# Sparse attention's value products in batches of two pairs, and the input embedding's side work begun at the first merged branch

## The chip, the core and the metric

The kernel runs on one core of one Trainium2 chip. Its time is device microseconds (us) of one execution. Below, PE is TensorE, DVE is VectorE, ACT is ScalarE, POOL is GpSimd, and SP is SyncE, which issues most DMAs.

## What is computed

A decoder trunk of two layers over 256 tokens of width 1024, in float32. Cut to what the change touches:

```python
for i in range(DEPTH):                       # 2 layers
    a = rmsnorm(h, norm_mix[i])
    proj = a @ w_in[i]                       # pool u | q | k, v | gates | GLA | merge gates
    y_a = pool_mixer(u_pool, ...)
    y_b = nsa_mixer(q_nsa, kv_nsa, g_nsa, positions, ...)   # partial rotary on q and k
    y_c = gla_mixer(...)
    merged = sum over k of sigmoid(g_k) * (y_k @ w_branch[i, k])
    h = h + merged @ w_out[i]
    h = h + square(relu(rmsnorm(h, norm_ffn[i]) @ w_ff1[i])) @ w_ff2[i]
    h = h + sigmoid(rmsnorm(h, norm_ple[i]) @ w_ple_gate[i]) * (p[i] @ w_ple_proj[i])

# inside nsa_mixer, for a head and a block of 128 queries
s = q @ k_sel.T;  o_slc = masked_softmax(s, ...) @ v_sel     # selected blocks
s = q @ kw.T;     o_win = masked_softmax(s, wmask) @ vw      # sliding window
o = g0 * o_cmp + g1 * o_slc + g2 * o_win
```

With 256 tokens every block is selected, so both softmaxes run over all earlier tokens.

## The kernel before

The matmuls with the weights are done in float32r, each as three products of a high and a low half (L1340, L1341, L1342). Weights come in units of 1 MB by DMA on the SP queue (`prefetch`, L181) into three raw buffers. ACT makes the high half (L187) and DVE the low half by a subtraction (L193); the low half frees the raw buffer for the next load.

Before anything is issued, the kernel writes a list `items` of matmul groups and hooks. A loop at the end walks through it, and the order in which it emits instructions is the order of each engine's queue; nothing is reordered later. A hook calls a function at its place in the list. After each pair of slots of a group the loop makes one step of weight preparation (`step`) and calls `pump`.

`pump` (L295) lets the side work advance. Side work is written as generators: `rope_setup` (sine and cosine of the positions, layer 0 only), `pool_gen`, `att_gen`, `gla_gen` and `emb_gen`. Each call of `pump` lowers the counter of every generator by one and then resumes one generator that is due, the first of the list; `yield 3` means that it is due again three calls later. So side generators compete for the calls: when one takes a call, another waits for the next. `finish(name)` runs what is left of one generator at once.

`emb_gen` loads p of the layer (256 KB, L780), yields 9, then transposes it on PE (L786, four transposes) and splits it into halves (`split`: ACT L232, DVE L234). The product with `w_ple_proj` uses it after the branches are merged.

`att_gen` begins, in the function for the last k and v columns, when the gates' columns of both token tiles are there. Its second step transposes k and v (L452); k has by then been rotated by `rotate` (DVE L388 to L390), which needs the table of rope. Its last part runs over `work`, twelve score items: four for token tile 0 with two heads each, eight for token tile 1 with one head each; neighbours are the two kv groups. At step n it does up to three things in this order: `mix`, `turn(n-2)`, `scores(n)`. `scores` makes a 128x512 tile of scores on PE (L569 to L571), its maximum on DVE (L575, L577), four or two exponentials on ACT (L581), and weighs it by the sums and the gate on DVE (L512 to L515). `turn` transposes that tile on PE (L592) and copies it to SBUF. `mix` multiplies the values with the transposed tiles of a pair of items (L615, sixteen instructions on PE for a pair; the first pair of a token tile also begins the sum with the compressed blocks' product, L606).

In layer 0, while rope is computed, the groups of the items "a" and "b" (the GLA output gate) are evacuated by a tanh on ACT and a product on DVE (L851 and L852, L857 and L858). The sine of rope (L380, L381) needs another table on ACT than tanh.

Of the kernel before, what the change touches and what calls it, by code (L numbers as in the profile page):

```python
# [115 lines left out]
def trunk(tc, x, p, positions, norm_mix, w_in, pool_w, pool_scale, cmp_pos_k, cmp_w_k, cmp_pos_v,  # L116
# [10 lines left out]
    with es:  # L127
# [14 lines left out]
        def wt(dt=F32):  # L142
            return wp.tile([128, 512], dt, tag="w", name=nm("w"))

        def ps():
            return pp.tile([128, 512], F32, tag="ps", name=nm("ps"))
# [83 lines left out]
        def split(q, scale=1.0):  # L230
            hi, lo = wt(F32R), wt(F32R)
            act(hi, q, AF.Copy, scale=scale)  # L232
            if scale == 1.0:
                tt(lo, q, hi.bitcast(F32), op=ALU.subtract)  # L234
            else:
                stt(lo, q, scale, hi.bitcast(F32), op0=ALU.mult, op1=ALU.subtract)
            return hi, lo
# [54 lines left out]
        def start(name, gen):  # L292
            sides.append([name, gen, 0])
# [134 lines left out]
        def att_gen(L, i):  # L428
# [128 lines left out]
            work = [(0, g, (2 * a, 2 * a + 1)) for a in range(2) for g in range(2)]  # L557
# [3 lines left out]
            def scores(n):  # L561
                t, g, hs = work[n]
                nk = 128 * (t + 1)
                q = ps()
                for a, hd in enumerate(hs):
                    o = q[:, a * 256:(a + 1) * 256].rearrange("p (b k) -> p b k", b=2) if t == 0 else q
                    A = slice(hd * 128, (hd + 1) * 128)
                    kh, kl = (k.rearrange("p (b k) -> p b k", b=2)[:, :, 0:128] if t == 0 else k for k in kz[g])
                    mm(o, qT[t][0][:, A], kh, start=True, stop=False)  # L569
                    mm(o, qT[t][0][:, A], kl, start=False, stop=False)  # L570
                    mm(o, qT[t][1][:, A], kh, start=False, stop=True)  # L571
                na = 512 // nk
                qv = q.rearrange("p (a k) -> p a k", a=na)
                dv = qv[:, :, nk - 128:nk]
                tt(dv, dv, causal[:, None, :].to_broadcast([128, na, 128]), op=ALU.add)  # L575
                mx = small(4, "mx", 4)
                nc.vector.tensor_reduce(mx[:, 0:na], qv, axis=AX.X, op=ALU.max, negate=True)  # L577
                e = wt()
                c = (g * 4 + hs[0]) * 2
                for a in range(na):  # L580
                    act(e[:, a * nk:(a + 1) * nk], q[:, a * nk:(a + 1) * nk], AF.Exp, bias=mx[:, a:a + 1],  # L581
                        accum_out=sums[t][:, c + a:c + a + 1])
                th = L.gate[t].rearrange("p (n j) -> p n j", j=3)[:, g * 4 + hs[0]:g * 4 + hs[-1] + 1, 1:3]
                weigh(e.rearrange("p (n b k) -> p n b k", n=len(hs), b=2),
                      sums[t][:, c:c + na].rearrange("p (n b) -> p n b", b=2), th)
                st[n] = e

            def turn(n):
                e = st[n]
                q = ps()  # L590
                for a in range(4):
                    nc.tensor.transpose(q[:, a * 128:(a + 1) * 128], e[:, a * 128:(a + 1) * 128], ident)  # L592
                s = wt()
                if n % 2:
                    act(s, q, AF.Copy)
                else:
                    nc.vector.tensor_copy(s, q)
                st[n] = s
# [3 lines left out]
            def mix(n):  # L602
                t, _, hs = work[n]
                if n in (0, 4):
                    oT.append(ps())
                    mm(oT[t], vbd, pbd[t], start=True, stop=False)  # L606
                o = oT[t][:, hs[0] * 128:(hs[-1] + 1) * 128]
                end = n + 2 == len(work) or work[n + 2][0] != t
                for br in range(2):
                    for b in range(t + 1):  # L610
                        for g in range(2):
                            G = slice(g * 64, (g + 1) * 64)
                            s = st[n + g].rearrange("p (n b k) -> p n b k", b=2, k=128)
                            rhs = s[:, :, br] if t == 0 else s[:, br, b]
                            mm(o[G].rearrange("p (n k) -> p n k", k=128) if t == 0 else o[G],  # L615
                               L.v[b][:, 256 + br * 128 + g * 64:256 + br * 128 + (g + 1) * 64], rhs,
                               start=False, stop=end and br == 1 and b == t)
                st[n] = st[n + 1] = None
                if end:
                    L.yB.append([split(oT[t], 0.5)])  # L620

            la, lb = 2, 4
            for n in range(len(work) + lb + 1):
                if n > lb and (n - lb) % 2:
                    mix(n - lb - 1)
                if la <= n < len(work) + la:
                    turn(n - la)
                if n < len(work):
                    scores(n)
                yield 3  # L630
# [147 lines left out]
        def emb_gen(L, i):  # L778
            s = wt()
            load(s.rearrange("q (t c) -> q t c", t=2), p[i, 0].rearrange("(t q) c -> q t c", q=128))  # L780
            yield 9
            q = ps()
            for t in range(2):
                for k in range(2):
                    c = slice(t * 256 + k * 128, t * 256 + (k + 1) * 128)
                    nc.tensor.transpose(q[:, c], s[:, c], ident)  # L786
            L.pT = split(q)


        def layer(i):  # L790
            L = Box()
# [6 lines left out]
            def hook(fn, *a):  # L798
                items.append(Hook(lambda: fn(*a)))
# [104 lines left out]
            else:  # L904
# [4 lines left out]
                items.append(ck[0][1])  # L909
                items.append(cq[1].pop(0))  # L910
                hook(norm_s, 1, kmix)
            hook(lambda: start("emb", emb_gen(L, i)))
            if i == 0:
                hook(lambda: late_start())
            items.extend(cq[1] + ck[1])
# [3 lines left out]
            def feed(c):  # L919
                c0, n, post = feeds[c]  # L920
                for gs in chunk(kmix, two(wi, c0, n), post, n):
                    items.extend(gs)

            def gm(br, ns=(0, 1)):
                for n in ns:
                    for gs in chunk(kmix, two(wi, C_GM + br * D + n * 512), post_gm(br, n)):
                        items.extend(gs)

            def branch(br, name, attr, first, ns=(0, 1)):
                for n in ns:  # L930
                    if br == 1:

                        wr = w_branch[i, br][:, n * 512:(n + 1) * 512].rearrange("(g i d) n -> g d i n", g=2, i=4)
                        u = unit([(slice(g * 64, g * 64 + 64), wr[g]) for g in range(2)])
                    else:
                        u = col_unit(w_branch[i, br], 0, n * 512, 512)
                    for t in range(2):
                        box = Box()

                        def post(t=t, n=n, box=box):  # L940
                            T = L.T[br, t, n]
                            stt(T, T, 1.0, box.ps, op0=ALU.add, op1=ALU.mult)
                            if first:
                                L.T["m", t, n] = T
                            else:
                                m = L.T["m", t, n]
                                tt(m, m, T, op=ALU.add)
                        pairs = [(s, (lambda t=t, s=s: lhs_of(getattr(L, attr)[t], s))) for s in range(4)]
                        items.append(Group(u, pairs, (box, 512), True, True, post))


            for c in SEQ:
                if c in feeds:
                    feed(c)
                elif c in "GHI":
                    gm("GHI".index(c))
                elif c == "g":
                    hook(finish, "pool")
                    branch(0, "pool", "yA", True)
                elif c == "h":  # L960
                    hook(finish, "att")
                    branch(1, "att", "yB", False)
                elif c == "i":
                    hook(finish, "gla")
                    branch(2, "gla", "yC", False)
# [199 lines left out]
        for i in range(DEPTH):  # L1165
            layer(i)
# [144 lines left out]
        for it in items:  # L1311
# [4 lines left out]
            box, n = it.acc  # L1316
# [56 lines left out]
```

## Time and profile before

| | |
|---|---|
| time, median of 3 runs | 917.88 us (917.86 to 918.08) |
| profiled execution | 917.47 us, span 915.7 us |
| mean granted clock of TensorE | 0.997 |
| PE busy | 905.3 us (99%) |
| DVE busy | 672.6 us (73%) |
| ACT busy | 486.2 us (53%) |
| POOL busy | 23.5 us (3%) |
| DMA | 160.02 MB, mean 175 GB/s |

The span is the time from the first to the last instruction that the profiler saw; the execution's own time is 1.8 us longer. Busy times can overlap on PE, since matmuls are pipelined: the distance from one start to the next says what a matmul takes of the span.

### The profile page before, as it was taken

The page shows a single profiled execution, that of the slowest core. Times are in us where ns is not written, and L with a number is a line of the kernel's source. Part 1 is how long each engine was busy: PE and PEld are TensorE (multiplying, and loading weights), DVE is VectorE, ACT ScalarE, POOL GpSimd, SP SyncE. Part 2 cuts the span into 40 slices and gives each one's busy share as a digit, 9 for nine tenths or more (in the row PEclk, how much of TensorE's full clock was granted, in tenths as well). Part 3 has the DMA queues.
Part 4 walks back from the last instruction along what each step waited for, and adds up shares of the span by engine and source line. Part 5 has one row for each costly group of instructions (what it writes and reads, how often), then busy time and mean ns, then how long its engine had stood idle before and what let it go on. Part 6 is the DMA issues. An engine that isn't in the chain of part 4 may idle for free.

```text
span 915.7 us, 12762 instructions
## 1 busy us (share of the span) xinstructions
PE 905.3 (99%) x4865; PEld 760.9 (83%) x4865; DVE 672.6 (73%) x1204; ACT 486.2 (53%) x838; POOL 23.5 (3%) x53
## 2 busy tenths in 40 slices
PE   9999999999999999999999999999999999999996
PEld 6988888788888888888889888878888888888885
DVE  5887877799567766666876877778985776666675
ACT  6665556454464544544665554645445565444553
POOL 1000000000000000000100000000000000000003
PEclk9999999999999999999999999999999999999998
DMA  8696453445535655555358825445553565555531
GB/s 273 198 286 201 138 161 116 121 155 189 180 138 197 229 199 199 187 184 184 99 154 268 238 94 183 139 149 128 163 192 106 180 233 184 184 185 189 197 143 46
DMA packets 92486, 160.02 MB, mean 175 GB/s; under 512 B 11756, under 2 KB 20616, under 8 KB 92424
## 3 DMA queue, kind: packets, MB, share of 16 engines
q1 hardware_dynamic: 92248, 159.13, 52.9%
q8 instruction: 38, 0.62, 0.3%
q14 instruction: 24, 0.20, 0.1%
q10 hardware_dynamic: 176, 0.07, 0.0%
HBM read 158.14 MB, written 1.05 MB: 174 GB/s over the span
## 4 chain that ended last, share of the span: by engine, by line
PE 95%; DVE 3%; DMA 1%; ACT 1%; issue 1%; ACTq 0%; DVEq 0%
PE ps L1340 21%; PE ps L1342 21%; PE ps L1341 21%; PE ps L1328 13%; PE ps L1330 7%; PE ps L615 1%; DVE lo L193 1%; PE ps L592 1%; PE ps L247 1%; DMA raw<-in_w_in 1%; PE ps L571 1%; PE ps L569 1%; PE ps L570 1%; PE ps L227 1%; PE ps L748 1%
## 5 line engine op out<-in xcount | busy, mean ns | idle before, releaser
L193 DVE TENSOR_TENSOR lo<-raw,hi 128x1024 fp32r<-128x1024 f32 (+1 forms) x296 | 340.9, 1179 | 41.7 <-ACT hi L187 39.6
L1340 PE MATMUL ps<-hi,w 128*128 128x512 f32 (+3 forms) x952 | 367.7, 386 | 0.5 <-ACT w L1301 0.5
L1342 PE MATMUL ps<-hi,w 128*128 128x512 f32 (+3 forms) x952 | 359.8, 378 | 0.0
L1341 PE MATMUL ps<-lo,w 128*128 128x512 f32 (+3 forms) x952 | 359.7, 378 | 0.0
L187 ACT ACTIVATE hi<-raw 128x1024 fp32r<-128x1024 f32 (+1 forms) x296 | 291.1, 1025 | 87.0 <-PE ps L1342 31.5
L1342 PEld LDWEIGHTS ps<-hi,w 128*128 128x128 f32 x952 | 178.9, 188 | 34.1
L1340 PEld LDWEIGHTS ps<-hi,w 128*128 128x128 f32 x952 | 179.0, 188 | 33.2 <-issue 1.4
L1341 PEld LDWEIGHTS ps<-lo,w 128*128 128x128 f32 x952 | 179.1, 188 | 30.5 <-DVE lo L1293 0.3
L1328 PE MATMUL ps<-w,hi 128*128 128x512 f32 x512 | 130.4, 392 | 0.0
L1328 PEld LDWEIGHTS ps<-w,hi 128*128 128x128 f32 x512 | 92.1, 189 | 16.3
L1330 PEld LDWEIGHTS ps<-w,lo 128*128 128x128 f32 x512 | 70.0, 190 | 5.1
L1330 PE MATMUL ps<-w,lo 128*128 128x256 f32 x512 | 71.6, 283 | 0.0
L1038 DVE TENSOR_TENSOR w<-w,ps 128x256 f32<-128x256 f32 x64 | 26.9, 420 | 57.3 <-ACT w L1037 57.3
L581 ACT ACTIVATE w<-ps,mx 128x128 f32<-128x128 f32 (+1 forms) x64 | 26.2, 417 | 78.9 <-DVE mx L577 57.5
L1037 ACT ACTIVATE w<-ps 128x256 f32<-128x256 f32 x64 | 24.2, 382 | 57.1 <-PE ps L1328 57.1
L232 ACT ACTIVATE w<-w 128x512 fp32r<-128x512 f32 x36 | 22.8, 632 | 56.2 <-DVE w L1040 50.5
L234 DVE TENSOR_TENSOR w<-w,w 128x512 fp32r<-128x512 f32 x36 | 24.9, 693 | 25.2 <-ACT w L232 25.2
L256 ACT ACTIVATE w<-ps,cols 128x128 fp32r<-128x128 f32 x64 | 17.4, 395 | 33.7 <-PE ps L247 33.7
L232 ACT ACTIVATE w<-ps 128x512 fp32r<-128x512 f32 x22 | 13.1, 596 | 36.2 <-PE ps L227 22.5
L512 DVE TENSOR_SCALAR sums<-sums 128x2 f32<-128x2 f32 (+1 forms) x24 | 4.1, 170 | 31.6 <-ACT w L581 31.6
L258 DVE SCALAR_TENSOR_TENSOR w<-ps,cols,w 128x128 fp32r<-128x128 f32 x64 | 17.3, 343 | 8.5 <-ACT w L256 8.5
L1040 DVE SCALAR_TENSOR_TENSOR w<-w 128x512 f32<-128x512 f32 x32 | 22.1, 692 | 1.1
(231 smaller groups left out, 677.6 us busy)
## 6 DMA issues: line engine op xcount, KB each, us to landing
raw<-in_w_ff SPq DMA_DIRECT2D x64, 1024.0 KB, 5.8
raw<-in_w_in SPq DMA_DIRECT2D x42, 1024.0 KB, 5.2
raw<-in_w_branch SPq DMA_DIRECT2D x8, 1024.0 KB, 5.3
raw<-in_w_out SPq DMA_DIRECT2D x8, 1024.0 KB, 5.1
raw<-in_w_ple_gate SPq DMA_DIRECT2D x8, 1024.0 KB, 5.2
raw<-in_w_in SPq DMA_DIRECT2D x8, 528.0 KB, 3.8
raw<-in_w_branch SPq DMA_DIRECT2D x8, 512.0 KB, 6.1
raw<-in_w_in SPq DMA_DIRECT2D x4, 560.0 KB, 5.2
```

What stands on the lines that cost most here:

```text
L187: act(hi, u.raw[:, a:b, :], AF.Copy)
L193: tt(lo, u.raw[:, a:b, :], hi.bitcast(F32), op=ALU.subtract)
L232: act(hi, q, AF.Copy, scale=scale)
L234: tt(lo, q, hi.bitcast(F32), op=ALU.subtract)
L581: act(e[:, a * nk:(a + 1) * nk], q[:, a * nk:(a + 1) * nk], AF.Exp, bias=mx[:, a:a + 1], accum_out=sums[t][:, c + a:c + a + 1])
L1037: act(zc, q[:, 256:512], AF.Copy)
L1038: tt(zc, zc, q[:, 0:256], op=ALU.add)
L1328: mm(box.ps, w, x, start=(it.first and s == 0), stop=(it.last and s == 3))
L1330: mm(box.ps[:, 0:256], w, x[:, 0:256], start=False, stop=False)
L1340: mm(box.ps, ah, wh, start=(it.first and j == 0), stop=False)
L1341: mm(box.ps, ah, wl, start=False, stop=False)
L1342: mm(box.ps, al, wh, start=False, stop=(it.last and j == last))
```

## The change

Two edits. In `att_gen`, `mix` is called for two neighbouring pairs of score items in one step, four items at a time, at n = 7, 11 and 15, where it was called for one pair at n = 5, 7, 9, 11, 13 and 15. The loop of steps is one shorter. In `layer`, the hook that starts `emb_gen` moves from behind the first q, k and v groups to the first merged branch, ahead of `finish("pool")`. The lines between the two places are numbered one higher after the change.

```diff
@@ -619,10 +619,11 @@
-            la, lb = 2, 4
-            for n in range(len(work) + lb + 1):
-                if n > lb and (n - lb) % 2:
+            la, lb = 2, 6
+            for n in range(len(work) + 4):
+                if n > lb and (n - lb) % 4 == 1:
                     mix(n - lb - 1)
+                    mix(n - lb + 1)
                 if la <= n < len(work) + la:
                     turn(n - la)
                 if n < len(work):
@@ -909,7 +910,6 @@
                 items.append(ck[0][1])
                 items.append(cq[1].pop(0))
                 hook(norm_s, 1, kmix)
-            hook(lambda: start("emb", emb_gen(L, i)))
             if i == 0:
                 hook(lambda: late_start())
             items.extend(cq[1] + ck[1])
@@ -955,6 +955,7 @@
                 elif c in "GHI":
                     gm("GHI".index(c))
                 elif c == "g":
+                    hook(lambda: start("emb", emb_gen(L, i)))
                     hook(finish, "pool")
                     branch(0, "pool", "yA", True)
                 elif c == "h":
```

PE's queue at step n = 5 in layer 0, before. The w tiles of L615 are the values and the turned tiles of items 0 and 1, that of L592 is the weighed tile of item 3, and L569 to L571 are the scores of item 5.

```order
L1342 MATMUL ps_1447<-hi_1259,w_224 128x512
L606 MATMUL ps_1506<-w_811,vbd_973 128x512
L615 MATMUL ps_1506<-w_1333,w_390 64x256
L615 MATMUL ps_1506<-w_1401,w_390 64x256
L615 MATMUL ps_1506<-w_1333,w_390 64x256
L615 MATMUL ps_1506<-w_1401,w_390 64x256
L592 MATMUL ps_1512<-con,w_1413 128x128 x4
L569 MATMUL ps_1519<-w_817,w_899 128x512
L570 MATMUL ps_1519<-w_818,w_899 128x512
L571 MATMUL ps_1519<-w_817,w_900 128x512
```

The same place after the change.

```order
L1343 MATMUL ps_1436<-hi_1248,w_224 128x512
L592 MATMUL ps_1495<-con,w_1402 128x128 x4
L569 MATMUL ps_1502<-w_806,w_888 128x512
L570 MATMUL ps_1502<-w_807,w_888 128x512
L571 MATMUL ps_1502<-w_806,w_889 128x512
```

The products of the first pair have left; the transposes of item 3 stand directly behind the weight matmuls. The first pair now stands at step n = 7, together with the second (items 0 to 3, then the turn of item 5 and the scores of item 7):

```order
L1343 MATMUL ps_1603<-hi_1350,w_157 128x512
L606 MATMUL ps_1627<-w_800,vbd_962 128x512
L615 MATMUL ps_1627<-w_1322,w_390 64x256
L615 MATMUL ps_1627<-w_1390,w_390 64x256
L615 MATMUL ps_1627<-w_1322,w_390 64x256
L615 MATMUL ps_1627<-w_1390,w_390 64x256
L615 MATMUL ps_1627<-w_1448,w_390 64x256
L615 MATMUL ps_1627<-w_1500,w_390 64x256
L615 MATMUL ps_1627<-w_1448,w_390 64x256
L615 MATMUL ps_1627<-w_1500,w_390 64x256
L592 MATMUL ps_1641<-con,w_1509 128x128 x4
L569 MATMUL ps_1648<-w_806,w_888 128x512
```

In layer 1 PE's queue is changed in the same way at both steps. ACT's queue in layer 0, before, from the tanh of L851 for token tile 0. The names rp and rope are the angles and the table of rope, and hi is a high half of weights.

```order
L851 ACTIVATE w_472<-ps_522,st_287 128x248
L187 ACTIVATE hi_590<-raw_533 128x560
L187 ACTIVATE hi_601<-raw_533 128x560
L851 ACTIVATE w_519<-ps_569,st_302 128x248
L187 ACTIVATE hi_617<-raw_554 128x560
L377 ACTIVATE rp_419<-rp_415 128x16
L380 ACT_TABLE_LOAD
L380 ACTIVATE rope<-rp_419 128x2x8
L381 ACTIVATE rope<-rp_415 128x2x8
L187 ACTIVATE hi_634<-raw_554 128x560
...
L828 ACT_TABLE_LOAD
L828 ACTIVATE gate_728<-ps_688,st_287 128x24
```

The same stretch after the change (L852 is the tanh that was L851).

```order
L852 ACTIVATE w_471<-ps_513,st_287 128x248
L187 ACTIVATE hi_581<-raw_524 128x560
L377 ACTIVATE rp_411<-rp_407 128x16
L380 ACT_TABLE_LOAD
L380 ACTIVATE rope<-rp_411 128x2x8
L381 ACTIVATE rope<-rp_407 128x2x8
L187 ACTIVATE hi_596<-raw_524 128x560
L852 ACT_TABLE_LOAD
L852 ACTIVATE w_510<-ps_560,st_302 128x248
L187 ACTIVATE hi_611<-raw_546 128x560
L187 ACTIVATE hi_623<-raw_546 128x560
```

The sine with its table load, which stood behind the second tanh, now stands ahead of it, and the second tanh has a table load of its own. The table load that stood ahead of the gates (L828) is gone.

## Rows read from the trace of the kernel before

**Rows 1.** Waits of TensorE; columns: engine, line, releaser, total us, times, longest.

```profile
PE ps L1234 <- DVE w L1229: 1.5, 1, 1.5
PE ps L1340 <- ACT w L1301: 0.5, 1, 0.5
PE ps L452 <- DVE w L390: 0.2, 1, 0.2
```

**Rows 2.** Timeline of TensorE, 141 to 195 us: start, us, instruction, count.

```profile
141.63 0.60 PE L592 MATMUL ps<-con,w 128*128 128x128 f32 x4
141.98 0.48 PE L569 MATMUL ps<-w,w 128*128 128x512 f32 x1
...
183.06 0.39 PE L1341 MATMUL ps<-lo,w 128*128 128x512 f32 x1
183.29 0.39 PE L1342 MATMUL ps<-hi,w 128*128 128x512 f32 x1
183.61 0.44 PE L748 MATMUL ps<-w,w 128*64 128x128 f32 x4
...
185.19 0.39 PE L751 MATMUL ps<-w,w 128*64 128x128 f32 x4
185.50 0.50 PE L1340 MATMUL ps<-hi,w 128*128 128x512 f32 x1
...
193.01 1.09 PE L615 MATMUL ps<-w,w 128*64 128x128 f32 x16
194.03 0.66 PE L592 MATMUL ps<-con,w 128*128 128x128 f32 x4
```

**Rows 3.** Timeline of TensorE, layer 0, step n=5 of att_gen.

```profile
131.63 1.02 PE L606 MATMUL ps<-w,vbd 128*128 128x512 f32 x2
132.58 1.08 PE L615 MATMUL ps<-w,w 128*64 128x256 f32 x8
133.60 0.66 PE L592 MATMUL ps<-con,w 128*128 128x128 f32 x4
134.01 0.47 PE L569 MATMUL ps<-w,w 128*128 128x512 f32 x1
```

**Rows 4.** Timeline of VectorE: last instructions of items 1, 3 and 11.

```profile
119.31 0.69 DVE L515 TENSOR_TENSOR w<-w,sums 128x512 f32<-128x512 f32 x1
...
132.46 0.69 DVE L515 TENSOR_TENSOR w<-w,sums 128x512 f32<-128x512 f32 x1
...
188.71 0.69 DVE L515 TENSOR_TENSOR w<-w,sums 128x512 f32<-128x512 f32 x1
```

**Rows 5.** Timeline of TensorE, layer 0, turn of item 1.

```profile
120.15 0.63 PE L592 MATMUL ps<-con,w 128*128 128x128 f32 x4
```

**Rows 6.** Timeline of ScalarE, 47 to 61 us; in brackets idle time and releaser.

```profile
47.54 0.47 ACT L851 ACTIVATE w<-ps,st 128x248 f32<-128x248 f32 x1 [3.04 <-DVE a L849]
...
49.88 0.47 ACT L851 ACTIVATE w<-ps,st 128x248 f32<-128x248 f32 x1 [0.75 <-DVE a L849]
...
51.56 0.21 ACT L377 ACTIVATE rp<-rp 128x16 f32<-128x16 f32 x1 [0.65 <-DVE rp L376]
51.79 1.28 ACT L380 ACT_TABLE_LOAD   x1
...
53.31 2.55 ACT L187 ACTIVATE hi<-raw 128x560 fp32r<-128x560 f32 x3
56.90 2.01 ACT L187 ACTIVATE hi<-raw 128x1024 fp32r<-128x1024 f32 x2 [1.03 <-DMA raw<-in_w_in]
```

**Rows 7.** Chain that ended last, 30 to 66 us: start, us, piece.

```profile
32.58 7.05 DMA raw<-in_w_in
...
41.74 0.49 ACT w L232
42.25 0.41 DVE w L234
```

**Rows 8.** Busy time by stretch, 6.0 to 8.4 us; last column GB/s.

```profile
6.00:8.40 2.40, 2.40 (x13) 1.69 (x12) 1.04 (x3) 0.37 (x1) 0.00 (x0) 1.00 1.00 356
```

**Rows 9.** Timeline of VectorE, from 57 us.

```profile
57.12 3.48 DVE L193 TENSOR_TENSOR lo<-raw,hi 128x1024 fp32r<-128x1024 f32 x3
```

## The prediction

> **What bounds the kernel now.** I read the page's first part, then the waits of TensorE (PE), then its timeline from start to start. PE is busy for 905.3 of 915.7 us, and all its waits with a named cause are three, 2.2 us together [rows 1]; two of them are from the start of the program, and the third is in front of L452, the transposes of k and v. So PE's own queue sets the end. An edit counts for the time that it takes from or adds to PE, and for each place where PE comes to an instruction before its operand is there. A busy DVE or ACT is worth nothing by itself, only through the moment at which it hands something to PE. Two places are touched: the steps of att_gen, and the stretch of layer 0 up to L452.
>
> **Fewer batches of value products: -1.8 us.** Three batches in each layer are joined to another one, six in all; the products stay the same. A batch is entered at a price: the first product of a run begins 0.32 us after the last 512-wide matmul (183.29 to 183.61 [rows 2]), whose pitch is otherwise 0.23 (183.06 to 183.29). That is 0.09. Two batches of sixteen take 2 x 1.02 = 2.04 (132.58 to 133.60 [rows 3], and the same for sixteen 128-wide ones, 193.01 to 194.03 [rows 2]); a run of 32 of the same height, eight groups of four in the linear attention (L748 and L751), takes 1.89 (183.61 to 185.50 [rows 2]). That is 0.15. Four transposes behind products take 0.41 (133.60 to 134.01 [rows 3]), alone 0.35 (141.63 to 141.98 [rows 2]): 0.06. Together 0.30 for each of six. If the 0.15 of the run of 32 doesn't carry over to L615, 0.9 is left; more than 2.0 I see no row for. I take 1.8, since the run of 32 has the same form.
>
> **The turn of item 3 loses the work in front of it: +3.4 us.** At n=5 PE did mix(0) and then turn(3). In layer 0 mix(0) filled 131.63 to 133.60, 1.97 us [rows 3]. What turn(3) transposes is the weighed exponential of item 3, and the last instruction that writes it, L515 on DVE, ends at 132.46 + 0.69 = 133.15 [rows 4]: hidden, with 0.45 to spare. With mix(0) gone to n=7, PE stands in front of the transposes at 131.63. How fast a released transpose starts is seen at turn(1), which waits already now: L515 ends at 119.31 + 0.69 = 120.00 [rows 4], L592 starts at 120.15 [rows 5], so 0.15. The wait is 133.15 + 0.15 - 131.63 = 1.67 us, with scores(5) and all of PE's queue behind it. Layer 1 has the same pattern at 580.77 with 0.05 less to spare, which gives 1.72; together 3.4. Nothing in the change brings item 3 forward: its chain on DVE and ACT has the same instructions in the same order, and the products have nothing on either engine until the split at the end. The bounds are 0 (item 3 ready 1.7 us sooner) and 3.9 (all of mix(0), twice). The other two turns that lose a batch in front of them have room: turn(11)'s operand is ready at 188.71 + 0.69 = 189.40 [rows 4] for a start at 194.03 [rows 2], 4.6 us, of which the batch was 1.0; turn(7) has more. The batches that now come later keep four weight tiles for two steps longer, and the pool of 47 has emb's tile less to hold until the branch.
>
> **The side work of the embedding moves: +1.1 and +0.45 us, both in layer 0.** Its four transposes cost PE 0.35, as the four of [rows 2], and 0.1 for the slower first matmul behind them. Before, that lay ahead of L452, where PE waits for DVE, so it was partly free; now it is paid behind. PE comes to L452 0.45 earlier and waits that much longer. In layer 1 there is no such wait, and the place makes no difference. The p load and the split then fall where PE has no wait and the result is needed only at the end of the branches, so I cost them at nothing; without that cover it would be the 0.9 of the split.
>
> The rest comes through rope. Each pump slot runs one due step, and while emb waited in the list it took turns that rope now gets, so rope's last part, with the table load for the sine, moves in front of the second tanh of L851 (the order of ACT above). Before, the load for the sine (51.79, 1.28 us) came behind both tanhs (47.54 and 49.88), and the load back at L828 had room [rows 6]. Now the second tanh has on its path: the first tanh and DVE's work up to the clamp, about 1.5 from 47.54 (0.48, 0.41, and three rope steps of 0.2); L377 0.21; a load of 1.28; the two sines 0.3; one 560-wide high half 0.6; the second load 1.28; its own 0.48. It ends 47.54 + 1.5 + 4.15 = 53.2 instead of 50.35, 2.8 later. From that go two reliefs. The split of emb stood in the chain with 0.49 + 0.41 and a gap of 0.2 [rows 7]; in its place the tanh of L857 of 0.47 is left, so 0.65. And the 256 KB of p were ahead of the 1 MB load that took 7.05 from its issue [rows 7]; at the 356 GB/s that loads side by side reach here [rows 8] they are 0.7, and they delay the load by that if it shares the engines with them throughout. So the second tanh is late by 2.8 - 1.34 = 1.45. Behind it stands the low half that frees a raw buffer, and behind that the load whose landing released ACT at 56.90 [rows 6]. Its low halves are the second and third of the DVE run at 57.12 [rows 9], which had some 0.35 of room. So DVE comes to L390, and PE to L452, 1.1 later. The bounds: 0 (the loads queue otherwise, or the room is larger) and 1.8 (the p load cost the others nothing).
>
> **Sum.** -1.8 + 3.4 + 1.1 + 0.45 = +3.15 on the profiled execution's 917.47, 920.6. That execution lies 0.41 under the median of the runs shown, 917.88; against the median the change gives **921.0**. What a measurement here can tell from no change is 0.2%, 1.84 us: 916.04 to 919.72.
>
> A rule that speaks against the change: a table load here takes 1.28, and the instruction behind it starts without a gap, as that in front ended without one [rows 6]. By the Trainium skill (ScalarE: Activation LUTs, What ACT_TABLE_LOAD costs) a switch costs the load of about 1283 ns and a drain of about 1380 ns besides; the trace agrees with the first number and shows no drain at 51.79. By that rule the sum would be 2.76 higher, since two switches would stand in the chain.
>
> **The rivals.**
> The other side: DVE's lag. DVE and ACT run several us behind PE, and emb's split and load leave the front. If the relief is 1.7 us at turn(3) in both layers, and keeps L452 free as well, both waits are gone: -1.8 - 0.2 [rows 1] = -2.0, 915.9. It decides from 1.67 us on. For it: the split and the load really go. Against it: by the rows they give 1.3 at most, far ahead of 131 us, and the table load takes it back. 0.06.
> Rope is harmless: the move of the sine's table load falls in room that I don't see, and L452 no longer waits, but turn(3) does: -1.8 + 3.4 - 0.2 = +1.4, 919.3, within 0.2%. For it: the first relief is sure; against it: ACT's order, and a chain without gaps from 50 to 65 us. 0.12.
> A switch of tables costs more where ACT has work in flight: by the nearest row as much again as the load, 2 x 1.28, 923.6. Against it: no such gap at 51.79. The page named above has this drain. 0.03.
> The forecast itself has the rest, 0.79, with its own range 919.9 (rope's 1.1 is 0) to 922.3 (rope 1.8, the batches save 1.2).
>
> **How the numbers follow.** The range 919.0 to 922.3 takes in the forecast and the harmless rope and leaves out the other side and the dear switch. Faster by over 0.2% is the other side, 0.06; within it, the harmless rope, 0.12; slower, 0.82.
>
> **What would show it.** Right: in both layers L592 at n=5 waits about 1.7 us for L515; none at turns 7 and 11; runs of 32 value products in about 1.89; on ACT two table loads some 2 us apart near 50 us, the landing that released ACT at 56.90 comes 1 to 2 us later, and L452 waiting 1.5 to 2.5 us for L390; PE's granted clock as before. Wrong: no wait at n=5, which would mean that DVE was not what held turn(3); L452 without a wait; a wait at a place not named here, such as for a raw load behind the emb load at the branch.

## The result and the profile after

The changed kernel takes 922.78 us (median of 6 runs, 921.15 to 924.89); the kernel before took 917.94 beside it (917.16 to 918.47). The ratio is 1.0053, 95% interval 1.0039 to 1.0067: slower by 4.8 us, where +3.15 was forecast, and above the forecast's range. Its single runs are spread over 3.7 us, those of the kernel before over 1.3.

The waits of TensorE (PE) in the changed kernel (engine, line, releaser, total us, times, longest), which answer to [rows 1]:

```profile
PE ps L452 <- DVE w L390: 3.1, 2, 2.7
PE ps L592 <- DVE w L515: 3.1, 2, 1.5
PE ps L1235 <- DVE w L1230: 1.5, 1, 1.5
PE ps L1341 <- ACT w L1302: 0.5, 1, 0.5
```

The two waits that were forecast are there, and no other is new. Now each of them. PE's timeline at step n = 5 in layer 0, then in layer 1, then DVE's at the same place, as [rows 3, 4]:

```profile
136.59 0.39 PE L1343 MATMUL ps<-hi,w 128*128 128x512 f32 x1
138.52 0.63 PE L592 MATMUL ps<-con,w 128*128 128x128 f32 x4 [1.54 <-DVE w L515]
...
586.65 0.39 PE L1343 MATMUL ps<-hi,w 128*128 128x512 f32 x1
588.56 0.63 PE L592 MATMUL ps<-con,w 128*128 128x128 f32 x4 [1.52 <-DVE w L515]
```

```profile
137.68 0.69 DVE L515 TENSOR_TENSOR w<-w,sums 128x512 f32<-128x512 f32 x1
```

From start to start it is 1.93 and 1.91 where a 512-wide matmul takes 0.23, so 1.70 and 1.68 are lost: 3.4, as forecast. L515 ends at 138.37, and the transposes start 0.15 later. The bracket says 1.5, since it counts from the modelled end of the matmul in front: a loss on PE is read from start to start.

The joined batches, in PE's timeline of the changed kernel:

```profile
154.51 1.95 PE L615 MATMUL ps<-w,w 128*64 128x256 f32 x16
156.39 0.66 PE L592 MATMUL ps<-con,w 128*128 128x128 f32 x4
...
185.34 1.97 PE L615 MATMUL ps<-w,w 128*64 128x128 f32 x32
187.24 0.66 PE L592 MATMUL ps<-con,w 128*128 128x128 f32 x4
```

A joined run takes 1.88 and 1.90 to the next start, where two took 2.04; the 0.15 that was forecast is there.

What was underrated is L452. PE's timeline in layer 0, against a start of the transposes at 65.05 and 65.50 before:

```profile
64.14 0.39 PE L1343 MATMUL ps<-hi,w 128*128 128x512 f32 x1
65.01 0.33 PE L452 MATMUL ps<-con,w 128*128 128x128 f32 x1 [0.48 <-DVE w L390]
68.00 0.90 PE L452 MATMUL ps<-con,w 128*128 128x128 f32 x3 [2.66 <-DVE w L390]
...
69.55 0.63 PE L1343 MATMUL ps<-hi,w 128*128 128x512 f32 x1
69.97 0.63 PE L1341 MATMUL ps<-hi,w 128*128 128x512 f32 x1
70.40 0.63 PE L1342 MATMUL ps<-lo,w 128*128 128x512 f32 x1
...
73.81 0.42 PE L1342 MATMUL ps<-lo,w 128*128 128x512 f32 x1
74.07 0.40 PE L1343 MATMUL ps<-hi,w 128*128 128x512 f32 x1
```

Two losses are to be seen. PE stands for 0.64 and 2.90 us (0.87 less 0.23, 2.99 less 0.09), 3.5 where it was 0.35. And behind the wait the same matmuls have a pitch (start to start) of 0.43 in place of 0.23, until 73.8. The stretches of this execution say why (length, busy time of PE, PEld, DVE, ACT, POOL, then the granted clock, DMA share, GB/s):

```profile
66.00:67.00 1.00, 0.00 (x0) 0.00 (x0) 0.97 (x6) 0.62 (x2) 0.00 (x0) 1.00 1.05 403
67.00:67.30 0.30, 0.00 (x0) 0.00 (x0) 0.30 (x4) 0.30 (x1) 0.00 (x0) 0.55 1.04 382
67.30:68.00 0.70, 0.01 (x1) 0.01 (x1) 0.67 (x5) 0.70 (x2) 0.00 (x0) 0.50 1.12 311
68.00:73.40 5.40, 5.40 (x17) 4.42 (x18) 5.37 (x8) 1.24 (x2) 0.00 (x0) 0.50 0.92 182
73.70:75.00 1.30, 1.30 (x9) 1.03 (x9) 1.29 (x4) 0.06 (x1) 0.00 (x0) 0.94 0.86 283
136.00:139.00 3.00, 1.46 (x10) 0.99 (x9) 1.83 (x5) 1.62 (x7) 0.00 (x0) 1.00 1.05 391
586.00:589.00 3.00, 1.48 (x10) 1.00 (x8) 1.79 (x5) 1.66 (x8) 0.00 (x0) 1.00 1.05 391
```

PE's clock went to its lower level, 1.2 for 2.4 GHz, while PE stood at L452, and stayed there until about 73.8, some 6.8 us, with PE busy throughout from 68.00 on. Start by start against the same matmuls in a run at full clock, the 18 pitches from 68.00 on took 2.7 us more. With 3.4 for the turns, 3.2 for L452's standing and -1.7 for the batches this makes 7.6; the profiled span is 7.4 longer (923.1 for 915.7; this execution took 924.89, the longest of the six). At the waits of L592 (last two rows) the clock stayed at its upper level.

ACT's timeline up to the second tanh and the next landing, as [rows 6]:

```profile
43.51 2.01 ACT L187 ACTIVATE hi<-raw 128x1024 fp32r<-128x1024 f32 x2 [0.92 <-DMA raw<-in_w_in]
47.73 0.47 ACT L852 ACTIVATE w<-ps,st 128x248 f32<-128x248 f32 x1 [2.21 <-DVE a L850]
...
49.41 1.28 ACT L380 ACT_TABLE_LOAD   x1
...
51.61 1.28 ACT L852 ACT_TABLE_LOAD   x1
52.91 0.47 ACT L852 ACTIVATE w<-ps,st 128x248 f32<-128x248 f32 x1
...
59.64 2.01 ACT L187 ACTIVATE hi<-raw 128x1024 fp32r<-128x1024 f32 x2 [3.25 <-DMA raw<-in_w_in]
```

The two table loads start 2.2 us apart, each within 0.02 us of the instructions ahead of it and behind it. The second tanh ends at 53.38, 3.0 later than before, where the forecast had 1.45; the landing comes at 59.64, 2.7 later, where it had 1 to 2.

### The profile page after: what moved, and what is told of

The parts are those of the page before. It is cut to its first block, busy times and chain, and to the rows that moved or that the text cites. A ratio compares the mean times of both kernels' runs of the same rounds, so it can differ in the third digit from the quotient of the medians.

```text
span 923.1 us, 12760 instructions
## 1 busy us (share of the span) xinstructions
PE 906.6 (98%) x4865; PEld 763.1 (83%) x4865; DVE 672.9 (73%) x1204; ACT 487.0 (53%) x838; POOL 23.6 (3%) x53
## 4 chain that ended last, share of the span: by engine, by line
PE 95%; DVE 3%; ACT 1%; DMA 1%; issue 0%; ACTq 0%; SPq 0%; DVEq 0%
PE ps L1341 22%; PE ps L1342 21%; PE ps L1343 21%; PE ps L1329 13%; PE ps L1331 7%; PE ps L615 1%; DVE lo L193 1%; PE ps L592 1%; PE ps L247 1%; ACT w L581 1%; PE ps L227 1%; PE ps L571 1%; PE ps L569 1%; PE ps L570 1%; DMA raw<-in_w_in 1%; PE ps L749 1%
```

## The experiments

All times are medians of 5 to 11 runs, with the kernel before run beside them (917.37 beside the first four, 917.67 beside the next four, then 917.46 beside three and 917.63 beside the last).

| run | us | against before | ratio, 95% interval |
|---|---|---|---|
| batches alone | 921.10 | +3.7 | 1.0027 to 1.0054 |
| emb move alone | 921.12 | +3.7 | 1.0023 to 1.0049 |
| emb move, pump calls kept | 917.33 | 0.0 | 0.9989 to 1.0007 |
| batches, later turns | 922.37 | +5.0 | 1.0045 to 1.0070 |
| changed kernel, pump calls kept | 919.16 | +1.5 | 1.0009 to 1.0026 |
| changed kernel, L452's wait filled | 921.90 | +4.2 | 1.0034 to 1.0059 |
| pump calls kept, first pair alone | 917.30 | -0.4 | 0.9986 to 1.0004 |
| pump calls kept, turn of item 3 later | 918.79 | +1.1 | 1.0003 to 1.0021 |
| changed kernel, sine later | 918.86 | +1.4 | 1.0008 to 1.0026 |
| first pair alone, 17 steps | 917.17 | -0.3 | 0.9987 to 1.0004 |
| pump calls kept, scores first at n = 5 | 918.86 | +1.4 | 1.0007 to 1.0024 |
| emb move, L452's wait partly filled | 919.37 | +1.7 | 1.0012 to 1.0030 |

**The two edits apart.** First the batches alone: the changed kernel with the hook of emb put back.

```diff
+            hook(lambda: start("emb", emb_gen(L, i)))
             if i == 0:
                 hook(lambda: late_start())
...
                 elif c == "g":
-                    hook(lambda: start("emb", emb_gen(L, i)))
```

> Only the batches of two pairs; emb starts where it did before. Theory (turn(3) loses its cover, rope's order costs the rest): the joined batches give 1.8, the two waits of L592 cost 1.5 to 1.7 each, so 3.1 to 3.4; sum +1.3 to +1.6, 919.2 to 919.5. L452 waits 0.2 to 0.4 as before, the clock stays at 1.00 from 20 to 900 us, and single runs lie within 1 us. Rival (the batches and the emb move act on each other, or the clock falls at the L592 waits): 921 or more, with a spread of several us.

Measured 921.10, 1.6 over the upper end, where the rival had put it. L592 waits as expected and L452 doesn't, but a wait is new. Its waits:

```profile
PE ps L592 <- DVE w L515: 3.1, 2, 1.6
...
PE ps L227 <- DVE w L770: 0.4, 2, 0.2
```

L227 are the transposes of the linear attention's output. From start to start they lose 1.45 in the two layers. In the kernel before the products of the pair at n = 13 took 1.0 of PE some 2 us ahead of them (193.01 [rows 2]; L227 at 195.92); here these products stand at n = 15, behind them. So a second place lost its cover (the work of PE that hides a wait), which the forecast had not looked at. With emb moved as well L227 doesn't wait (changed kernel, above): PE comes to it at 202.41, for 195.95 here. So the two edits are not additive; which step of emb makes the difference I didn't try. The tail behind the last matmul is 0.7 longer in this profile than in the others, and that stays open too.

The move of emb alone, which is the second half of the change's diff made in the kernel before:

> Only the move of emb; the value products are batched as before. Theory: the sine's table load ahead of the second tanh delays rope, L452 waits 2 to 3.5 us in all, and the granted clock falls behind that wait in some runs, each microsecond at half clock costing half a microsecond: 919.5 to 923.5, single runs spread over 2 us or more, waits of L592 at items 0 and 1 only, as before. Rival (the wait of L452 came with the batches, or the loads just landed late in one run): within 0.5 us of the kernel before.

921.12, as expected, though the runs spread over 1.7 us and not 2 or more; one run of five, with the highest mean clock, took 919.52. PE's timeline and the clock of its profile:

```profile
64.88 0.27 PE L452 MATMUL ps<-con,w 128*128 128x128 f32 x1
67.23 0.55 PE L452 MATMUL ps<-con,w 128*128 128x128 f32 x3 [2.08 <-DVE w L390]
```

```profile
66.00:67.20 1.20, 0.00 (x0) 0.00 (x0) 1.15 (x7) 1.20 (x2) 0.00 (x0) 1.00 1.09 340
67.20:68.40 1.20, 1.17 (x7) 1.04 (x8) 1.20 (x2) 0.59 (x1) 0.00 (x0) 1.00 1.33 248
68.40:71.90 3.50, 3.50 (x12) 2.83 (x11) 3.49 (x5) 0.69 (x1) 0.00 (x0) 0.51 1.30 236
71.90:73.00 1.10, 1.10 (x8) 0.91 (x7) 1.09 (x4) 0.00 (x0) 0.00 (x0) 0.99 1.08 379
```

The clock fell some 1.2 us after PE had gone on, and for some 3.4 us; by the starts that cost 1.6. PE's second start at L452 is 1.7 later than in the kernel before (65.50), where the forecast had 1.1.

**Is it rope's place in ACT's order?** The same move, with an empty generator that takes the two pump calls that emb had.

```diff
+        def pad_gen():
+            yield 9
...
+            if i == 0:
+                hook(lambda: start("pad", pad_gen()))
```

> The move of emb alone, but in layer 0 an empty generator takes the two pump calls that emb took, so ACT's order up to the gates is that of the kernel before, less emb's split. Theory (rope's place in ACT's order is the cause): one table load behind both tanhs and one ahead of the gates, L452 waits under 0.8 us, clock 1.00, 917.4 to 918.6. Rival (emb's own work or load taken out of the front is the cause): L452 waits 2 us or more, 919.5 or more.

917.33, the time of the kernel before. L452 waits 0.4. So neither emb's place nor its work in the front counts; what counts is who gets the pump calls. The same on the changed kernel:

> The changed kernel, but in layer 0 the empty generator takes emb's two old pump calls. Theory: L452 waits under 0.8 us and the clock stays at 1.00, the two waits of L592 at item 3 stay at 1.5 to 1.7, the joined batches give 1.3 to 1.8: 918.6 to 919.6, single runs within 1 us of each other, so 3 to 4 us under the changed kernel. Rival (the L452 wait is a matter of DVE's lag or of the loads): 921 or more.

919.16, in the middle, 3.6 under the changed kernel (3.35 with each against the kernel before beside it), and no wait at L452; the waits of L592 are unchanged:

```profile
PE ps L592 <- DVE w L515: 3.0, 2, 1.5
PE ps L1240 <- DVE w L1235: 1.4, 1, 1.4
PE ps L1346 <- ACT w L1307: 0.5, 1, 0.5
```

Then without the empty generator, only the sine put behind the second tanh again:

In `rope_setup` of the changed kernel:

```diff
+            yield 8
             lim = 3.1415925
             ts(r, r, lim, -lim, op0=ALU.min, op1=ALU.max)
```

> The changed kernel with one yield of 8 calls ahead of rope's last part, so the sine and its table load stand behind both tanhs again, with no empty generator. Theory (the place of the table load, not the pump calls as such, makes L452 wait): L452 waits under 0.8 us, clock 1.00, 918.6 to 919.6, as the run with the old pump calls kept. Rival (other steps of rope or emb's absence from the front make the wait): 921 or more.

918.86, as expected, and L452 waits nowhere. It is the place of rope's last part, the sine with its table load; emb's absence from the front is not the cause. The clamp ahead of the sine moved with it, and the table load by itself was not moved.

**What the wait costs, and what the clock.** Twelve products that nobody reads stand ahead of L452, in the changed kernel.

```diff
+            if i == 0:
+                busy, keep = ps(), aT[("mix", i), 0][0][0]
+                for _ in range(12):
+                    mm(busy, keep[:, 0:128], keep, start=True, stop=True)
             for kv in range(2):
                 src = (L.k, L.v)[kv]
```

> The changed kernel with twelve 128x512 products into an unread PSUM tile ahead of L452 in layer 0, 12 x 0.23 = 2.7 us of TensorE work where it would wait. Theory (the fall of the clock behind the wait is a cost of its own): L452 waits under 1 us, the granted clock stays at 1.00 between 60 and 80 us, 920.0 to 921.5, 1 to 2.5 below the changed kernel although PE does 2.7 us more. Rival (the fall of the clock costs nothing, as PE is ahead of DVE anyway, or it has another cause): 922.5 or more, or half clock as before.

921.90, single runs within 0.4 us (921.62 to 922.04), and the clock at 1.00 throughout. It is 0.4 over the range that I gave, since the products (2.7) were longer than what was left of the wait, which is gone altogether; the time is that of the kernel with the pump calls kept plus the 2.7. The median is 0.9 under that of the changed kernel, 0.6 with each against the kernel before beside it. But two of the six runs of the changed kernel (921.15 and 921.80) are as fast, and the intervals overlap: that useless work makes this kernel faster is not shown. What it plainly does is to narrow the spread, from 3.7 us to 0.4. With six products, on the move of emb alone:

> The move of emb alone, with six 128x512 products into an unread PSUM tile ahead of L452 in layer 0: 6 x 0.23 = 1.4 us, less than the 2.1 us that TensorE waits there without them, so they add nothing to the sum of work and wait. Theory (the fall of the clock is a cost beside the wait): L452 waits 0.5 to 1.2 us, the granted clock stays at 1.00 from 60 to 80 us, 919.3 to 920.0, 1 to 1.6 under the move alone. Rival (the wait alone is the cost): 920.8 to 921.3, as without the products, whatever the clock.

919.37, as expected, 1.75 under the move alone (2.0 with each against the kernel before beside it). The wait was not as expected, though: 1.9, since the first of the four transposes was free and the second stood from 65.33 to 67.48, 2.15 us, nearly the 2.35 without the products. PE's timeline and the clock:

```profile
63.97 1.53 PE L450 MATMUL ps<-w 128*128 128x512 f32 x6
65.33 0.27 PE L456 MATMUL ps<-con,w 128*128 128x128 f32 x1
67.48 0.55 PE L456 MATMUL ps<-con,w 128*128 128x128 f32 x3 [1.88 <-DVE w L390]
```

```profile
66.00:67.00 1.00, 0.00 (x0) 0.00 (x0) 0.96 (x6) 1.00 (x3) 0.00 (x0) 1.00 1.05 383
68.00:69.00 1.00, 1.00 (x6) 0.81 (x5) 1.00 (x2) 0.04 (x1) 0.00 (x0) 1.00 1.19 211
```

L452 goes on 0.25 later than in the move alone, and the kernel is 1.75 faster. That is not the wait, then; it is the clock, which in all eleven runs has a mean of 0.997 or 0.998 (0.995 to 0.997 in the move alone).

**The cover of turn(3).** All turns one step later, with the batches alone:

```diff
-            la, lb = 2, 6
+            la, lb = 3, 6
```

> The batches of two pairs with emb started as before, and every turn one step later (la 3 for 2). Theory: all transposes find their item ready, no L592 wait in either layer; the joined batches' 1.8 stays and the present 0.15 at turn(1) in each layer goes: 915.8 to 916.2. Rival (the later turns only move the wait to the batches or to a tile that is held longer, or the batches give nothing): 917.5 or more.

A miss, 922.37. L592 waits nowhere, but others do:

```profile
PE ps L227 <- DVE w L770: 2.4, 2, 1.2
PE ps L419 <- ACT w L411: 2.1, 4, 0.7
```

PE is so far ahead of DVE and ACT there that it stands at the next thing which one of them hands over: L419 are the pool branch's products, whose operand ACT evacuates (L411). Only the turn of item 3 later, with the pump calls kept:

```diff
                 if la <= n < len(work) + la:
-                    turn(n - la)
+                for m in {5: (), 6: (3, 4)}.get(n, (n - la,)):
+                    if 0 <= m < len(work):
+                        turn(m)
```

> As the changed kernel with the old pump calls kept, all batches of two pairs, and only the turn of item 3 moved from n = 5 to n = 6, behind which it is first needed at n = 7. Theory: no wait at item 3; all three joins in each layer pay, 1.35 together by what the run with the batches alone shows: 915.7 to 916.4. Rival (the wait moves to the step behind, as the later turns of all items did): 917.5 or more.

918.79: a miss by the same rule, 0.4 under the kernel with the wait, where 3 were expected. Its waits are 0.7 at L419 and 0.4 at L409, for the DMA of the pool's matrix. Half a cover, the scores of item 5 ahead of the turn at n = 5 alone:

```diff
+                if n == 5:
+                    scores(n)
                 if la <= n < len(work) + la:
                     turn(n - la)
-                if n < len(work):
+                if n < len(work) and n != 5:
                     scores(n)
```

> As the changed kernel with the old pump calls kept, and at n = 5 alone the scores of item 5 ahead of the turn of item 3. Theory (turn(3) lacks a cover of 1.55 us in each layer, whatever it is made of): the scores' 0.77 us cover half of it, L592 waits 0.7 to 0.9 in each layer, 1.5 us less than with the old pump calls kept alone: 917.3 to 918.0. Rival (the wait is a matter of PE's place among the steps, or scores(5) waits for its own tile): 919 or more.

The wait of L592 is halved, as expected (0.83), but the time is a miss and hardly moves: +1.4 against the kernel before, where the whole wait gave +1.5. Its waits:

```profile
PE ps L592 <- DVE w L515: 1.7, 2, 0.8
...
PE ps L419 <- ACT w L411: 0.7, 2, 0.3
```

From start to start L419 loses 1.2 more in the two layers. What PE wins at L592 it gives back there. The cover itself put back, with the first two pairs alone and only the pairs of token tile 1 joined:

```diff
-                if n > lb and (n - lb) % 4 == 1:
-                    mix(n - lb - 1)
-                    mix(n - lb + 1)
+                for m in {5: (0,), 7: (2,), 11: (4, 6), 15: (8, 10)}.get(n, ()):
+                    mix(m)
```

> As the changed kernel with the old pump calls kept, but the first two pairs stay alone at n = 5 and 7, and only the pairs of token tile 1 are joined (4 of 6 joins less one in each layer, so two in each). Theory: turn(3) has its cover back and waits under 0.2 us; two joins in each layer give 0.2 to 0.3 each, 0.8 to 1.2 together: 916.2 to 916.8. Rival (the joins give nothing, or another turn waits): 917.3 or more.

917.30, 0.4 under the kernel before, and turn(3) waits nowhere: what the batches had lost was the cover. The time is 0.5 over the range, so the two joins pay less than expected. (The diff is against the changed kernel with the pump calls kept, as the two above.) The starts of PE say -0.65 for the two joins that are left in each layer and +0.3 lost at L227. The same with 17 steps (`range(len(work) + 5)`):

> As the run with the first pair kept, with the loop of 17 steps as in the kernel before, so that the generators behind att_gen get their calls as before. Theory (the joined batch at n = 15 leaves L227, the next transposes, 0.1 to 0.2 us short in each layer, which one empty step gives back): 916.7 to 917.2. Rival (L227 has nothing to do with the steps): 917.3 as without.

917.17 is in the range of the theory, but against the kernel before beside it (-0.3) it is no better than without, and L227's loss is still there (0.36): the step isn't its cause. For no version does the 95% interval lie below 1: none is shown to be faster than the kernel before.

## Why the prediction was wrong

**The batches: -1.8, right.** By the starts of PE in the run with the pump calls kept, against the same without batches, six entries of 0.32 go (-1.9), six starts of L592 behind products become starts behind a matmul (-1.43 + 1.38), the pitches inside the longer runs cost 0.5 more, those of L592 0.3 less: -1.7.

**Turn(3): +3.4, right,** 1.70 and 1.68 where I gave 1.67 and 1.72. That it is the missing cover is shown by the runs with half of it and all of it. But three other orders gave little or nothing of the 3.4 back: PE then stands at other places (L227, L419, L409).

**L452: +1.55, wrong; it is 3.35 to 3.6** (changed kernel less the run with the pump calls kept, with each against the kernel before beside it, and by the medians). The mechanism is right: the sine with its table load ahead of the second tanh, shown by putting it back. The step that failed has two parts, and the clock is the larger. "PE's granted clock as before" was one of the things that I named as signs of being right, and I priced a wait as the time that PE stands. Behind this one the clock fell, for some 3.4 us in the move alone and 6.8 in the changed kernel, which cost 1.6 and 2.7 in the executions profiled. The six runs of the changed kernel go with it: 921.15 and 921.80 at a mean clock of 0.998, 922.36 to 923.37 at 0.996, 924.89 at 0.993. The two at 0.998, whose mean clock leaves no room for such a fall, are 3.2 and 3.9 above the kernel before, where the forecast had +3.15: of the 1.7 by which the median exceeds it, 1.0 to 1.6 is the clock by this estimate, and the rest is for the other part. With the clock held by the six products the move costs 1.7, 0.25 of it for the later start; with the fall, 3.7.

The other part: the reliefs of 1.34 that I took off, and 0.35 of room. "The 256 KB of p were ahead of the 1 MB load", for 0.7: the load that they preceded released ACT at the same time with p ahead of it (first row, the batches alone) and without (second row, the move with the pump calls kept). Over all profiles this ACT instruction starts at 39.46 to 39.73 in the three with p ahead and at 39.03 to 40.22 in the eleven without (median 39.47), so of the 0.7 hardly 0.2 can be seen. ACT's timelines:

```profile
39.46 1.06 ACT L187 ACTIVATE hi<-raw 128x1024 fp32r<-128x1024 f32 x1 [2.61 <-DMA raw<-in_w_in]
```

```profile
39.54 1.06 ACT L187 ACTIVATE hi<-raw 128x1024 fp32r<-128x1024 f32 x1 [3.36 <-DMA raw<-in_w_in]
```

The other relief, 0.65 for emb's split, was partly taken up by the next load, which ACT now waits for (0.92 at 43.51; no such wait before). The last L390 ahead of L452 ends at 65.45 in the kernel before, at 64.54 in the run with emb moved and the pump calls kept, and at 67.17 in the move alone (in all profiles with these orders of ACT: 65.17 to 65.45, 64.13 to 64.72, 67.12 to 67.94). So the sine's place costs 2.6 here, near the 2.8 that I reckoned, and all that leaves the front gives 0.9 in place of 1.34 and 0.35. L390 came 1.7 (move alone) to 2.5 later (changed kernel), and not 1.1; the upper bound that I gave, 1.8, holds for the first.

**The rivals.** The other side did not come: the front gave 0.9 us at L390, and both waits are there. Rope was not harmless. A switch of tables with a drain by the Trainium skill (ScalarE: Activation LUTs, What ACT_TABLE_LOAD costs): the trace shows the load's 1.28 twice, the instruction ahead of each ending 0.01 us before it and the next one starting 0.02 us behind it, so there is no drain here either. A fall of the clock was not among the rivals, and should have been, wherever a wait of PE is forecast.

## What to carry to other kernels

Before work is moved out of an engine's queue to be done in one piece, look at what the next instruction in that queue waits for: the moved work may be its cover, and the room is read from the end of its operand's last writer to its start. Side work that shares a turn-taking scheduler can't be moved alone; the calls that it no longer takes bring other work forward, here a table load into the middle of a chain. Price a wait of TensorE with the clock that may fall behind it, and if the wait can't be taken away, something to do for TensorE ahead of it can be cheaper than standing: with six products here it was, with twelve that is not shown.

## What the runs showed of the hardware

Six matmuls with no use, 1.4 us of them, made the move alone 1.75 us faster, by keeping the granted clock at its upper level; twelve, 2.7 us, held it as well and left the changed kernel no slower in the median, with single runs within 0.4 us in place of 3.7. The clock fell after PE had already gone on in one run (68.4 us, PE busy from 67.2) and while it stood in another (67.0, PE idle from 65.3). With the six matmuls ahead of it an idle stretch of 1.9 us (65.6 to 67.5) passed without a fall, and so did the 1.5 us at L592 (granted clock 1.00 in 136 to 139 and 586 to 589). A table load costs ACT 1.28 us with no gap around it, also when two of them are 2.2 us apart.
